# Last product of a hybrid decoder layer: weight sums of twelve of its twenty groups made during the third gating and the up projection and kept in DRAM, with one or two more buffers of each kind

## The chip, the cores and the metric

The kernel runs on one core of a Trainium2 chip. The metric is the device time of one execution in microseconds (us); lower is better. All arithmetic is in float32: a weight or an activation is split into a high part (the value rounded to fp32r, the type that TensorE takes here) and a low part (the rest), and each product is made of three matmuls, high by high, high by low and low by high.

The engines go by the profile's names: PE (TensorE), DVE (VectorE), ACT (ScalarE), POOL (GpSimd), SP (the queue that issues most DMAs).

## The reference

One decoder layer on 256 positions and 2048 channels. An input projection feeds three mixers (A a gated convolution, B a spatial gating, C sparse attention), each with its own output projection and a sigmoid gate; their gated sum goes through `w_o`, a norm and the residual. Then a feed-forward part:

```python
splits = _split_points()
...
    g_a, g_b, g_c = jnp.split(jax.nn.sigmoid(merge_g), 3, axis=-1)
    mixed = (g_a * y_a + g_b * y_b + g_c * y_c) @ w_o[l]
    x = x + rms_norm(mixed, norm_mix_post[l])
    h = rms_norm(x, norm_ffn_pre[l])
    u = causal_depthwise_conv(h @ w_up[l], ffn_conv_w[l], ffn_conv_b[l])
    u_g, u_v = jnp.split(u, 2, axis=-1)
    x = x + rms_norm((jax.nn.silu(u_g) * u_v) @ w_down[l], norm_ffn_post[l])
```

The last product is the one with `w_down`: 256 x 5632 by 5632 x 2048.

## The kernel before

**Stages in order of time:** input projections of the three mixers; gating and output projection of each branch (`branch(0)` for B, `branch(1)` for A, `branch(2)` for C, the "third gating"); the product with `w_o`; the up projection, 88 tiles `f` of 128 features (loop over `NFT`, two tiles a turn); the last product, in two halves of 1024 output columns (`Pair(0)`, `Pair(1)`).

**How a weight gets to PE.** SP loads 128x1024 values (512 KB) into a raw buffer `wraw` (five of them). ACT writes the high part into `whi` (four buffers), DVE subtracts and writes the low part into `wlo` (four buffers). PE then reads both. In the up projection a tile takes two such units, in the gating and in the `w_o` product one unit feeds 12 matmuls.

**The last product.** The 44 feature tiles are 20 in ten pairs (`EARLY`) and 24 alone (`PLAIN`). A plain tile is one unit and 12 matmuls of 128x512 into four PSUM banks `c`. A pair is a "group" (`quad`): one step of a fast matrix product with seven instead of eight block products, for which the four weight blocks of the pair are loaded as `b` and `a` (each 128x1024) and four sums of 128x512 are made of them on DVE, partly in place: `tt[L] = b[L]-a[U]`, `a[U] = a[U]-a[L]`, `tt[U] = b[L]-a[U]`, `b[U] = b[U]-tt[U]`. Then `b`, `a`, `tt` and the upper half of `b` (as `h4`, `l4`, one buffer each) are split, 3.5 units in all, and 21 matmuls follow, into `c` and the four side banks `p1`, `p5`, `p6`, `p7`. The sums of the activations are made ahead, in the up projection (`sums`). `combine` adds the side banks into the result buffer `res`, `result` adds the banks `c`, `weigh` multiplies by the norm's gain.

**What sets the order.** PE's order is set by `in_line`, ACT's and DVE's in the last product by `fixed`: each instruction is issued after the one before it on its engine, in the order of the program text. Elsewhere a scheduler sets the order from priorities; the splits of weights stand ahead of other work (`high_priority`). In `Pair(1)` the last six plain tiles are "kept": their weights are split ahead of time, four of them into buffers of activations no longer needed, and multiplied after everything else, bank by bank, so that each bank's tail (`result`, norm, `weigh`, residual, store) starts early. The residual waits in DRAM (`kept_y`) and is loaded near the end.

Of the kernel before, what the change touches and what calls it, by code (L numbers as in the profile page):

```python
# [30 lines left out]
D = 2048  # L31
T = 256
# [5 lines left out]
EARLY = [(0, 1), (2, 3), (4, 5), (6, 7), (8, 9), (11, 12), (13, 14), (15, 16), (17, 18), (19, 20)]  # L38
PLAIN = [*range(22, 33), 10, 21, *range(33, NFT)]
BA, BB, BC, BG = 2100, 2200, 2200, 2500  # L40
# [14 lines left out]
def block(ctx: ExitStack, tc: tile.TileContext, x, xf, fp, cst, rows, sgw, w1, w2, wf_a, wt_bv, wf_bu, wf_c,  # L55
# [5 lines left out]
    P0 = ctx.enter_context(tc.tile_pool(name="p0", bufs=1))  # L61
    PS = ctx.enter_context(tc.tile_pool(name="ps", bufs=4, space=PSUM))
# [192 lines left out]
    PZ.tile([128, 112], F32, name="fill")  # L255
# [3 lines left out]
    idn = P0.tile([128, 128], F32, name="idn")  # L259
# [62 lines left out]
    hT = P0.tile([128, KT, 2, T], R, tag="hT", name="hT")  # L322
# [24 lines left out]
    rh = PZ.tile([128, 2], F32, name="rh")  # L347
# [532 lines left out]
    mix = {}  # L880

    def branch(bi, act_of):

        for cb in range(4):
            pg = [PS.tile([128, 512], F32, tag="acc", name=f"pg{bi}{cb}{t}") for t in range(2)]
            for q in range(4):
                hs = granule(wt_g[(bi * 4 + cb) * 4 + q])
                for k in range(4 * q, 4 * q + 4):
                    hi, lo = hs[(k % 4) // 2]
                    c = slice((k % 2) * 512, (k % 2) * 512 + 512)  # L890
                    for t in range(2):
                        ts = slice(t * 128, t * 128 + 128)
                        mm_t(pg[t], hT[:, k, 0, ts], hT[:, k, 1, ts], hi[:, c], lo[:, c], k == 0, k == KT - 1)
                if q < 3:
                    pump(BUDGET)
# [9 lines left out]
            for q in range(2):  # L905
# [7 lines left out]
                for k in range(4 * q, 4 * q + 4):  # L913
                    hi, lo = hs[(k % 4) // 2]
                    c = slice((k % 2) * 512, (k % 2) * 512 + 512)
                    for t in range(2):
                        ts = slice(t * 128, t * 128 + 128)
                        mm_t(py[t], act[:, k, 0, ts], act[:, k, 1, ts], hi[:, c], lo[:, c], k == 0, k == 7)
                if q == 0:
# [28 lines left out]
    branch(2, lambda: Ct_box["t"])  # L948
    mh, ml = mix["h"], mix["l"]
# [10 lines left out]
    ss2 = PZ.tile([128, 2, 4], F32, tag="ss8", name="ss2")  # L960
# [72 lines left out]
    h2k = P0.tile([128, 4, 2, 1024], R, tag="hT", name="h2k")  # L1033
# [10 lines left out]
    for n, (cb, p) in enumerate(HELD):  # L1044
        for i in range(2):
# [4 lines left out]
            if (n, i) == (3, 1):  # L1050
                h2 = P0.tile([128, KT, 2, T], R, tag="hT", name="h2T")
# [79 lines left out]
    sums_of = [P2.tile([128, 2, 5, 3, 128], R, name="se")]  # L1131
    gh = [P2.tile([128, 11, T], R, tag="gh", bufs=4, name=f"gh{i}") for i in range(4)]
# [7 lines left out]
    rb2 = junk.bitcast(F32)  # L1140
    ones2 = small("ones2", (128, 128))
# [27 lines left out]
    def sums_at(j):  # L1169
        return sums_of[j // 5][:, 0, j % 5], sums_of[j // 5][:, 1, j % 5]  # L1170

# [30 lines left out]
    for i in range(NFT):  # L1202
        acc = []
        for v in range(2):
            f = 2 * i + v
            with tc.issue_after(pe_last[0]):
                pu = pu2[f] if f < 3 else ftile(wf_up[f], h2)
            s = P2b.tile([128, T], F32, tag="fs", bufs=2, name=f"fs{f}")
            fsum(pu, s, rb=rb2)
            a = small(f"fa{f}")  # L1210
# [21 lines left out]

    P2c = ctx.enter_context(tc.tile_pool(name="p2c", bufs=1))
    fin = P0.tile([128, 7168], F32, tag="hT", name="fin")
    res = fin[:, 0:4096].rearrange("p (t n) -> p t n", t=2)
    gain = fin[:, 4096:5120]
    turn = [0]

    def scratch():
        turn[0] ^= 1  # L1240
        return fin[:, 5120 + 1024 * turn[0]:6144 + 1024 * turn[0]]

    ss3 = PZ.tile([128, 2, 8], F32, name="ss3")
# [12 lines left out]
    def weights(src, into=None):  # L1256
        raw = fetch(src, 1024)
        hi, lo = (into[:, 0], into[:, 1]) if into is not None else ring(raw.name)
        high(hi, raw)
        rest(lo, raw, hi)  # L1260
        return hi, lo

    def ring(name):
        return P0.tile([128, 1024], R, tag="whi", bufs=4, name=f"whi{name}"), rests(f"wlo{name}")[:, 0:1024]

    class Pair:
# [27 lines left out]
        def quad(self, j):  # L1294

            k0, k1 = EARLY[j]
            last = j == len(EARLY) - 1
            b, a = (fetch(wt_dq[self.p, j][:, x:x + 1024], 1024) for x in (0, 1024))
            L, U = slice(0, 512), slice(512, 1024)
            nm = f"q{self.p}_{j}"  # L1300
            tt = scratch()
            (hb, lb), (ha, la), (ht, lt) = (ring(nm + x) for x in "bat")
            h4, l4 = (P2c.tile([128, 512], R, tag=tag, name=f"{tag}{nm}") for tag in ("h4", "l4"))
            high(hb, b)
            fixed(V, V.tensor_sub, tt[:, L], b[:, L], a[:, U])
# [3 lines left out]
            fixed(V, V.tensor_sub, tt[:, U], b[:, L], a[:, U])  # L1309
            high(ht, tt)  # L1310
            rest(la, a, ha)
            fixed(V, V.tensor_sub, b[:, U], b[:, U], tt[:, U])
            high(h4[:, L], b[:, U])
            rest(lt, tt, ht)
            rest(l4[:, L], b[:, U], h4[:, L])
            sh, sl = sums_at(j)
            s1, s2, s4 = ((sh[:, i], sl[:, i]) for i in range(3))
            for bank_, act, (h, l), c in (
                    (self.c[0][1], s4, (hb, lb), L), (self.c[0][0], g2(k1, H1), (hb, lb), U),
                    (self.p1, g2(k0, H1), (ha, la), L), (self.p5, s1, (ha, la), U),  # L1320
                    (self.p7, g2(k0, H2), (ht, lt), L), (self.p6, s2, (ht, lt), U),
                    (self.c[1][0], g2(k1, H2), (h4, l4), L)):
# [34 lines left out]
    NP, NQ, KEEP = len(PLAIN), len(EARLY), 6  # L1357


    first, second = Pair(0), None  # L1360
    i = 0
    for j in range(NQ):
        while i < 3 + (NP - 6) * j // (NQ - 1):
            first.plain(i)
            i += 1
        first.quad(j)
    for i in range(i, NP):
        first.plain(i)
    first.combine()
    second = Pair(1)  # L1370
    kept = []
    i = 0
    for j in range(NQ):
        while i < 3 + (NP - KEEP - 3) * j // (NQ - 1):
# [158 lines left out]
```

## Time and profile before

| | us |
|---|---|
| median of 3 runs | 1564.04 (1563.71 to 1564.49) |
| the profiled execution | 1564.15 |
| its span | 1562.4 |

The page gives each engine's busy time, the chain of work that ended last, and groups of instructions by line. Further views: the chain in order of time; windows (for each stretch its length, then PE, PEld, DVE, ACT and POOL busy us with the number of instructions, the clock granted to PE as a share of full speed, the DMA engines' busy share and GB/s); groups by line (busy us, mean ns of one, idle time just before and what ended it); DMA issues (queue, count, size, median us from issue to landing).

The stages by the chain and the groups: `branch(2)`'s output projection (`py<-whi,Ct`) runs from 631 to 751 us, the up projection's tiles from 877 to 1324 in the chain, the first half of the last product starts at 1325.7, the second at 1438.6. DVE's busy share by fifths of the page's forty slices:

```profile
PE   9999999999999999999999999999999999999997
DVE  7899999857866555465567998888888888888997
```

One digit is the busy share of a fortieth of the span in tenths. DVE is least busy in the middle, from about 430 to 820 us, where the gatings and the `w_o` product run.

### The profile page before, as it was taken

To read this page: it belongs to the slowest core of one execution; us is meant where nothing else is said; L and a number is where in the kernel's file an instruction comes from. 1 tells how busy PE (TensorE), PEld (TensorE's weight loads), DVE (VectorE), ACT (ScalarE), POOL (GpSimd) and SP (SyncE) were. 2 spreads that over 40 slices of the span, in tenths; PEclk is the share of its full clock that TensorE was granted. 3 is DMA by queue.
4 is the path that set the end of the run, shared out by engine and by line. 5 is a ranking of instruction groups with operands and counts; after the bars stand their busy time and mean duration, and the time that the engine had idled before them with its cause. 6 is when DMAs were issued, how large, how long until landed. Compare 5 with 4: busy or idle time off the path is not lost.

```text
span 1562.4 us, 22642 instructions
## 1 busy us (share of the span) xinstructions
PE 1551.2 (99%) x8178; PEld 1316.5 (84%) x8178; DVE 1244.8 (80%) x2370; ACT 889.3 (57%) x1442; POOL 19.2 (1%) x50
## 2 busy tenths in 40 slices
PE   9999999999999999999999999999999999999997
PEld 7888889888888787788888888888888888888885
DVE  7899999857866555465567998888888888888997
ACT  7654454447646675644455665565555555555663
POOL 1000020000000000000000000000000000000000
PEclk9999999999999999999999999999999999999999
DMA  9565556666764445466774666666666666666674
GB/s 377 182 197 185 193 177 215 197 192 180 234 201 161 151 147 169 156 189 188 243 245 144 215 193 196 195 190 196 191 190 197 194 193 195 200 208 202 215 236 156
DMA packets 85441, 307.96 MB, mean 197 GB/s; under 512 B 9808, under 2 KB 10832, under 8 KB 84304
## 3 DMA queue, kind: packets, MB, share of 16 engines
q1 hardware_dynamic: 83376, 297.84, 60.0%
q0 software_dynamic: 1520, 8.39, 1.5%
q8 instruction: 64, 1.05, 0.3%
q14 instruction: 49, 0.40, 0.1%
q10 hardware_dynamic: 432, 0.28, 0.1%
HBM read 301.23 MB, written 4.19 MB: 195 GB/s over the span
## 4 chain that ended last, share of the span: by engine, by line
PE 96%; DVE 2%; DMA 1%; issue 0%; ACT 0%; DVEq 0%; POOL 0%; ACTq 0%; POOLq 0%
PE ps L190 29%; PE ps L197 15%; PE pg L211 6%; PE pg L210 6%; PE pg L212 6%; PE pd0b L1282 5%; PE pd1a L1282 4%; PE py L211 3%; PE py L212 3%; PE py L210 3%; PE po L210 2%; PE po L211 2%; PE po L212 2%; PE pd0a L1282 2%; PE pd1b L1282 1%; PE pv L210 1%
## 5 line engine op out<-in xcount | busy, mean ns | idle before, releaser
L149 ACT ACTIVATE whi<-wraw 128x1024 fp32r<-128x1024 f32 x440 | 461.9, 1054 | 250.8 <-PE pg L212 95.8
L151 DVE TENSOR_TENSOR wlo<-wraw,whi 128x1024 fp32r<-128x1024 f32 (+1 forms) x187 | 226.4, 1216 | 156.5 <-ACT whi L149 155.8
L163 DVE TENSOR_TENSOR wlo<-wraw,whi 128x896 fp32r<-128x896 f32 (+1 forms) x506 | 325.8, 685 | 12.1 <-ACT whi L149 7.3
L190 PE MATMUL ps<-h2T,whi 128*128 128x512 f32 x1360 | 323.1, 389 | 0.0
L190 PEld LDWEIGHTS ps<-h2T,whi 128*128 128x128 f32 x1360 | 249.2, 188 | 46.8
L197 PEld LDWEIGHTS ps<-h2T,wlo 128*128 128x128 f32 x1360 | 167.0, 188 | 6.7
L197 PE MATMUL ps<-h2T,wlo 128*128 128x256 f32 x1360 | 168.9, 277 | 0.0
L190 PE MATMUL ps<-hT,whi 128*128 128x512 f32 x640 | 156.6, 391 | 0.0
L212 PE MATMUL pg<-whi,hT 128*128 128x512 f32 x384 | 150.9, 393 | 0.0
L211 PE MATMUL pg<-wlo,hT 128*128 128x512 f32 x384 | 150.7, 392 | 0.0
L232 ACT ACTIVATE t<-ps 128x256 f32<-128x256 f32 x125 | 47.4, 380 | 175.9 <-PE ps L190 175.9
L210 PE MATMUL pg<-whi,hT 128*128 128x512 f32 x384 | 147.3, 393 | 0.0
L190 PEld LDWEIGHTS ps<-hT,whi 128*128 128x128 f32 x640 | 115.8, 188 | 21.1
L493 DVE SCALAR_TENSOR_TENSOR cv<-hb,fps,cv 128x256 f32<-128x256 f32 x240 | 104.2, 475 | 0.0
L233 DVE TENSOR_TENSOR t<-ps,t 128x256 f32<-128x256 f32 x125 | 52.6, 421 | 50.4 <-ACT t L232 50.4
L197 PEld LDWEIGHTS ps<-hT,wlo 128*128 128x128 f32 x640 | 82.0, 188 | 4.5
L211 PEld LDWEIGHTS pg<-wlo,hT 128*128 128x128 f32 x384 | 72.1, 188 | 16.2 <-issue 1.1
L212 PEld LDWEIGHTS pg<-whi,hT 128*128 128x128 f32 x384 | 72.1, 188 | 15.1 <-issue 0.7
L197 PE MATMUL ps<-hT,wlo 128*128 128x256 f32 x640 | 84.3, 278 | 0.0
L210 PEld LDWEIGHTS pg<-whi,hT 128*128 128x128 f32 x384 | 71.8, 188 | 14.8 <-issue 0.3
L998 DVE TENSOR_TENSOR wlowraw<-wraw,whiwraw 128x1024 fp32r<-128x1024 f32 x44 | 53.2, 1222 | 11.6 <-ACT whiwraw L998 10.2
L998 ACT ACTIVATE whiwraw<-wraw 128x1024 fp32r<-128x1024 f32 x44 | 45.7, 1055 | 18.0 <-PE pd0b L1282 15.0
(1021 smaller groups left out, 2517.3 us busy)
## 6 DMA issues: line engine op xcount, KB each, us to landing
wraw<-in_wf_up_dram SPq DMA_DIRECT2D x176, 512.0 KB, 4.4
wraw<-in_wt_g_dram SPq DMA_DIRECT2D x96, 512.0 KB, 4.3
wraw<-in_wt_p_dram SPq DMA_DIRECT2D x48, 512.0 KB, 3.8
wraw<-in_wt_dn_dram SPq DMA_DIRECT2D x48, 512.0 KB, 4.2
wraw<-in_wt_dq_dram SPq DMA_DIRECT2D x40, 512.0 KB, 4.5
wraw<-in_wf_a_dram SPq DMA_DIRECT2D x32, 512.0 KB, 4.2
wraw<-in_wt_o_dram SPq DMA_DIRECT2D x32, 512.0 KB, 4.6
wraw<-in_wf_bu_dram SPq DMA_DIRECT2D x16, 512.0 KB, 3.9
```

Of the source, the lines that this page charges most:

```text
L149: S.activation(hi[:, :n], raw[:, :n], AF.Copy)
L151: V.tensor_sub(lo[:, :n], raw[:, :n], hi[:, :n].bitcast(F32))
L163: V.tensor_sub(*x)
L190: ins = PE.matmul(ps[:, :, ts], lhsT=ws[k // 8][0][:, c:c + 128], rhs=mov[:, k, :, ts], start=(k == 0 and not t), stop=(k == n - 1), skip_ ...
L197: ins = PE.matmul(ps[:, 1, ts], lhsT=ws[k // 8][1][:, c:c + 128], rhs=mov[:, k, 0, ts], start=False, stop=False, skip_group_check=True).ins
L210: PE.matmul(ps, lhsT=xh, rhs=hi, start=first, stop=False)
L211: PE.matmul(ps, lhsT=xh, rhs=lo, start=False, stop=False)
L212: return PE.matmul(ps, lhsT=xl, rhs=hi, start=False, stop=last).ins
L233: V.tensor_add(t1 if rb is not None else dst, ps[:, 0], t1)
L493: V.scalar_tensor_tensor(ca[:, j], hb[:, j, k:k + T], w(j, k), ca[:, j], op0=ALU.mult, op1=ALU.add)
L998: seq[eng] = [op(*args, **kw).ins]
L1282: ins = PE.matmul(bank, lhsT=a[x], rhs=w[y], start=first and j == 0, stop=last and j == 2).ins
```

## The change

For twelve of the twenty groups (five of the first half, seven of the second; letter Y in the strings below, Q is a group as before) the four sums are made earlier by `weight_sums`: POOL loads the group's blocks `b` and `a` into a buffer, DVE makes the four sums there, POOL writes them to a DRAM tile `made` (2560 columns a group). Eight groups are done in `branch(2)`, one buffer `wsum`, a step of the generator twice a granule; four in the up projection, two buffers (`early`, in place of activation tiles filled later), a step of both at every third tile. Two copies of one column per group, from a tile just written, hold the loads back until that point of the program. In the last product a made group is loaded as four pieces (three of 512 KB, one of 256), split like plain tiles, with no sums.

Besides: one more raw buffer, one more `whi` and one more `wlo` (in the space of `h2T`, on the right side of the memory, where `hT`, `idn`, `res` and the gain now lie), two scratch tiles in place of two halves of one tile, and the order of plain tiles, groups, results and kept tiles written out as the strings `FIRST` and `SECOND`.

```diff
+FIRST = "PPPYPPQPPYPPPQPPYPPQPPYPPQPPYPPQPP"
+SECOND = "PPPRRRRWPYWPPQWPWPYGPPQPPYPPQKPYKPYKPYKBPYKK"
+MADE = [(p, j) for p, steps in enumerate((FIRST, SECOND)) for j, c in enumerate(c for c in steps if c in "QY") if c == "Y"]
...
+    made = tc.dram_tile([max(len(MADE), 1), 128, 2560], F32, name="made")
+
+    def weight_sums(quads, room):
+
+        for n in quads:
+            p, j = MADE[n]
+            y = room(n)
+            L, U = slice(0, 512), slice(512, 1024)
+            b, a, t = y[:, 0:1024], y[:, 1024:2048], y[:, 2048:2560]
+            for x in (b, a):
+                V.tensor_copy(x[:, 0:1], now[0][:, 0:2].bitcast(F32)[:, 0:1] if now[0] is junk else now[0][:, 0:1].bitcast(F32))
+            G.dma_start(b, wt_dq[p, j][:, 0:1024])
+            G.dma_start(a, wt_dq[p, j][:, 1024:])
+            yield
+            yield
+            V.tensor_sub(t, b[:, L], a[:, U])
+            G.dma_start(made[n, :, 1024:1536], t)
+            yield
+            V.tensor_sub(a[:, U], a[:, U], a[:, L])
+            G.dma_start(made[n, :, 0:1024], a)
+            yield
+            V.tensor_sub(b[:, L], b[:, L], a[:, U])
+            yield
+            V.tensor_sub(b[:, U], b[:, U], b[:, L])
+            G.dma_start(made[n, :, 1536:], b)
+            yield
+            yield
...
+                if bi == 2:
+                    next(making, None)
+                    next(making, None)
...
+    making = [weight_sums(range(MIXER + x, len(MADE), 2), lambda n: early[(n - MIXER) % 2]) for x in range(2)]
...
+            if (2 * i + v) % 3 == 0:
+                for steps in making:
+                    next(steps, None)
...
+    raws_of = cycle(tagged("wraw", 5, F32) + [spare(2)])
+    whi = cycle(tagged("whi", 4, R) + [spare(0)])
+    wlo = cycle([lambda name, dt=R: rests(name)[:, 0:1024]] * 4 + [spare(1)])
+    scratch = cycle([extra(0)] + [extra(1)])
...
         def quad(self, j):
...
+            if (self.p, j) in MADE:
+                m = made[MADE.index((self.p, j))]
+                b, a, t = (weights(x) for x in (wt_dq[self.p, j][:, 0:1024], m[:, 0:1024], m[:, 1024:2048]))
+                return self.seven(j, b, a, t, split(load(m[:, 2048:], 512)[:, 0:512], (fourth("h4"), fourth("l4"))))
```

P is a plain tile, R a result, W a `weigh`, G the load of the gain, K a kept tile, B the load of the residual. PE's instructions are the same in number and kind.

**In the order of the instructions.** First DVE in the third gating, at the third of the eight groups (`wsum` is the buffer of the sums, `wlo` the low part of a weight unit, `Ct` the output of mixer C). Before:

```order
L151 TENSOR_TENSOR wlo_6350<-wraw_6347,whi_6349 128x1024
L151 TENSOR_TENSOR wlo_6356<-wraw_6353,whi_6355 128x1024
L151 TENSOR_TENSOR wlo_6386<-wraw_6383,whi_6385 128x1024
L151 TENSOR_TENSOR wlo_6392<-wraw_6389,whi_6391 128x1024
L151 TENSOR_TENSOR wlo_6422<-wraw_6419,whi_6421 128x1024
L845 TENSOR_TENSOR Ct<-O_5651,Ct 128x4x128
```

And now:

```order
L158 TENSOR_TENSOR wlo_6386<-wraw_6383,whi_6385 128x1024
L898 COPY wsum_6413<-wlo_6386 128x1 x2
L158 TENSOR_TENSOR wlo_6421<-wraw_6418,whi_6420 128x1024
L903 TENSOR_TENSOR wsum_6413<-wsum_6413 128x512
L906 TENSOR_TENSOR wsum_6413<-wsum_6413 128x512
L158 TENSOR_TENSOR wlo_6427<-wraw_6424,whi_6426 128x1024
L909 TENSOR_TENSOR wsum_6413<-wsum_6413 128x512
L911 TENSOR_TENSOR wsum_6413<-wsum_6413 128x512
L158 TENSOR_TENSOR wlo_6461<-wraw_6458,whi_6460 128x1024
L852 TENSOR_TENSOR Ct<-O_5657,Ct 128x4x128
```

Two copies and four subtractions now stand between the units' rests; one unit's rest stands between the copies, behind which POOL issues the loads, and the first subtraction, which needs them.

Second POOL at the same group (`made` is the DRAM tile, `rnmp` a row of gains that the `w_o` product's end uses). These rows are new but for `rnmp`, which had only the loads of `x` behind it in this stage:

```order
L912 DMA made<-wsum_6215 128x1024
L1003 DMA rnmp<-in_rows_dram 128x2048
L899 DMA wsum_6413<-in_wt_dq_dram 128x1024
L900 DMA wsum_6413<-in_wt_dq_dram 128x1024
L904 DMA made<-wsum_6413 128x512
L907 DMA made<-wsum_6413 128x1024
L912 DMA made<-wsum_6413 128x1024
```

POOL's queue, nearly empty before, now carries five DMAs a group, and `rnmp` and `x` are issued behind those of the groups ahead.

Third SP in the second half of the last product, where kept tile, plain tile and group follow each other (`in_wt_dn_dram` holds plain and kept tiles, `in_wt_dq_dram` the groups' blocks). Before, with its next kept tile:

```order
L103 DMA wraw_14658<-in_wt_dn_dram 128x1024
L103 DMA wraw_14662<-in_wt_dn_dram 128x1024
L103 DMA wraw_14680<-in_wt_dn_dram 128x1024
L103 DMA wraw_14698<-in_wt_dq_dram 128x1024
L103 DMA wraw_14700<-in_wt_dq_dram 128x1024
L103 DMA wraw_14744<-in_wt_dn_dram 128x1024
```

And now:

```order
L1336 DMA u_14853<-in_wt_dn_dram 128x1024
L1336 DMA u_14857<-in_wt_dn_dram 128x1024
L1336 DMA u_14875<-in_wt_dq_dram 128x1024
L1336 DMA u_14881<-made 128x1024
L1336 DMA u_14887<-made 128x1024
L1336 DMA u_14893<-made 128x512
L1336 DMA u_14921<-in_wt_dn_dram 128x1024
```

A group's two loads became four, three of them from `made`; the one plain tile between two kept tiles takes one load as before.

More of the change, by code (lines that the diff above doesn't have):

```diff
@@ L880, in block @@
     mix = {}
+    made = tc.dram_tile([max(len(MADE), 1), 128, 2560], F32, name="made")
[23 more added lines that the diff above has]
+            yield
+    MIXER = min(len(MADE), 8)
+    making, now = weight_sums(range(MIXER), lambda n: P1.tile([128, 2560], F32, tag="wsum", name=f"wsum{n}")), [None]
     def branch(bi, act_of):
@@ L1131, in block @@
     sums_of = [P2.tile([128, 2, 5, 3, 128], R, name="se")]
+    early = [P2.tile([128, 11 * T], F32, tag=tag, bufs=4, name="made" + tag) for tag in ("gh", "gl")]
     gh = [P2.tile([128, 11, T], R, tag="gh", bufs=4, name=f"gh{i}") for i in range(4)]
@@ L1254, in rest, with cycle, take, spare @@
         fixed(V, V.tensor_sub, lo, x, hi.bitcast(F32))
-    def weights(src, into=None):
[L1257 to L1264, printed above, removed]
+    def cycle(makers):
+        n = [0]
+        def take(name, *args):
+            n[0] += 1
+            return makers[(n[0] - 1) % len(makers)](name, *args)
+        return take
+    def spare(x):
+        return lambda name, dt=R: P2d.tile([128, 1024], dt, tag=f"y{x}", name=name)
+    def extra(x):
+        return lambda name, dt=R: P2c.tile([128, 1024], dt, tag=f"x{x}", name=name)
+    def tagged(tag, bufs, dtype):
+        return [lambda name, dt=dtype: P0.tile([128, 1024], dt, tag=tag, bufs=bufs, name=name)] * bufs
+    raws_of = cycle(tagged("wraw", 5, F32) + [spare(2)])
+    whi = cycle(tagged("whi", 4, R) + [spare(0)])
+    wlo = cycle([lambda name, dt=R: rests(name)[:, 0:1024]] * 4 + [spare(1)])
+    scratch = cycle([extra(0)] + [extra(1)])
+    count = [0]
+    def load(src, n=1024):
+        count[0] += 1
+        to = raws_of(f"u{count[0]}", F32)
+        nc.sync.dma_start(to[:, :n], src)
+        return to
+    def split(x, into=None):
+        hi, lo = into or (whi(f"h{count[0]}"), wlo(f"l{count[0]}"))
+        high(hi, x)
+        rest(lo, x, hi)
+        return hi, lo
+    def weights(src, into=None):
+        return split(load(src), into)
+    def fourth(tag):
+        return P2c.tile([128, 512], R, tag=tag, name=f"{tag}_{count[0]}")
     class Pair:
@@ L1389, in block @@
                 G.dma_start(yb[:, t], kept_y[:, t])
-        for x in range(0 if j < NQ - 5 else 1 if j < NQ - 1 else KEEP - 4):
-            k = NP - KEEP + len(kept)
-            into = None
-            if j < NQ - 1:
-                kt = P2.tile([128, 11, T], R, tag=("gh", "gl")[j % 2], bufs=4, name=f"kept{k}")
-                into = kt[:, 0:8].rearrange("p (a b) c -> p a (b c)", a=2)
-            kept.append((PLAIN[k], weights(wt_dn[1, k], into)))
-    assert i == NP - KEEP and len(kept) == KEEP
+        elif c == "K":
+            keep()
+        else:
+            second.quad(j)
+            j += 1
     second.combine()
+    P2d.tile([128, 120], F32, name="fill2")
     for t in range(2):
```

133 lines of the change are left out of this document (77 added, 56 removed).

## The prediction

> **What bounds the kernel now.** I read the page first, then the chain that ended last in order of time, then the windows of the last product, then the groups by line.
>
> ```profile
> span 1562.4 us, 22642 instructions
> PE 1551.2 (99%) x8178; PEld 1316.5 (84%) x8178; DVE 1244.8 (80%) x2370; ACT 889.3 (57%) x1442; POOL 19.2 (1%) x50
> PE 96%; DVE 2%; DMA 1%; issue 0%; ACT 0%; DVEq 0%; POOL 0%; ACTq 0%; POOLq 0%
> ```
>
> PE is busy in 99% of the span and is 96% of the chain; DVE and DMA share the last 3%. A busy PE may still be waiting inside a matmul whose end is modelled, so I look at the pace. In the chain in order of time (start, length, what, matmuls merged) the last product reads:
>
> ```profile
> 1325.74 9.52 PE pd0b L1282 x42
> 1337.98 7.48 PE pd0b L1282 x33
> ...
> 1438.62 9.52 PE pd1a L1282 x42
> ...
> 1523.55 5.22 DMA wraw<-in_wt_dq_dram
> 1536.40 17.04 PE pd1a L1282 x75
> ```
>
> 9.52/42 and 7.48/33 are both 0.2267 us for one matmul. Each half of the product has 24 plain tiles of 12 matmuls and 10 groups of 21, together 498, so 112.9 us at this pace. The first half runs from 1325.74 to 1438.62, which is 112.88: PE lost nothing there. The second starts at 1438.62 and its last matmul ends at 1553.44, 114.82 later; a last matmul shows about 0.16 beyond its step, so the half lost 114.82 - 0.16 - 112.88 = **1.8 us**. The windows say where (first the length, then each engine's busy us with its count, clock, DMA share, GB/s):
>
> ```profile
> 1460.00:1480.00 20.00, 20.00 (x90) 16.57 (x89) 19.90 (x25) 11.44 (x12) 0.00 (x0) 1.00 0.72 238
> ...
> 1510.00:1520.00 10.00, 10.00 (x46) 8.19 (x45) 8.88 (x11) 5.63 (x7) 0.00 (x0) 1.00 0.78 251
> 1520.00:1530.00 10.00, 9.44 (x42) 7.36 (x41) 8.04 (x10) 5.49 (x6) 0.00 (x0) 1.00 0.69 219
> 1530.00:1540.00 10.00, 9.84 (x42) 7.22 (x41) 9.93 (x13) 5.14 (x6) 1.09 (x2) 1.00 0.19 53
> 1540.00:1550.00 10.00, 10.00 (x46) 8.29 (x45) 5.54 (x14) 3.34 (x8) 0.00 (x0) 1.00 0.41 170
> ```
>
> Two windows hold 42 matmuls where the neighbours hold 46: 8 x 0.2267 is again 1.8 us. Ahead of them DVE is busy for 19.90 of 20 us, and the chain runs through DVE and one load of a group's weights: DVE has used up its lead, and the load was issued late because its buffer was held by the sums made in place. What can be won by relieving DVE in this product is therefore 1.8 us, 0.1%. From PE's end at 1553.44 the span has 9.0 us more, in instructions that the change leaves as they are.
>
> **The change, part by part.** All durations are of the profiled execution: 1564.15 us, span 1562.4; the median of the runs is 1564.04, 0.1 lower.
>
> PE's matmuls are the same in number, kind and, but for some transposes of the third gating, order: no gain and no loss of its own.
>
> *DVE and ACT in the product.* The rows (mean ns of one, then idle before):
>
> ```profile
> L998 DVE TENSOR_TENSOR wlowraw<-wraw,whiwraw 128x1024 fp32r<-128x1024 f32 x44 | 53.2, 1222 | 11.6 <-ACT whiwraw L998 10.2
> L998 ACT ACTIVATE whiwraw<-wraw 128x1024 fp32r<-128x1024 f32 x44 | 45.7, 1055 | 18.0 <-PE pd0b L1282 15.0 <-PE ps L190 2.6 <-PE pd0a L1282 0.3
> L998 DVE TENSOR_TENSOR fin<-wraw,wraw 128x512 f32<-128x512 f32 x40 | 27.4, 685 | 3.1 <-DMA wraw<-in_wt_dq_dram 3.0
> ```
>
> A made group loses four subtractions of 0.685 us, 2.7 us; seven of them in the second half take 19.2 us from DVE. For the stretch from 1440 to 1540 that is
>
> ```profile
> 1440.00:1540.00 100.00, 99.28 (x434) 80.73 (x434) 94.83 (x111) 59.97 (x68) 1.09 (x2) 1.00 0.63 203
> ```
>
> a fall from 94.8 of 100 us to 75.6. ACT's work stays. The 1.8 us of PE's wait goes: **-1.8**.
>
> *DMA in the product.* A made group is loaded as three loads of 512 KB and one of 256 instead of two of 512: 0.79 MB more, 12 times. What is late next is therefore a transfer, and the place is the end of the second half, where plain tile, made group and kept tile follow each other four times: 2.75 MiB = 2.88 MB in 33 matmuls, 7.48 us, so 385 GB/s (before, 2.10 MB, 280 GB/s). The nearest rows for what the queues can give:
>
> ```profile
> 12.00:16.00 4.00, 4.00 (x20) 3.30 (x19) 4.00 (x10) 3.93 (x9) 0.00 (x0) 1.00 1.04 416
> ...
> wraw<-in_wt_dq_dram SPq DMA_DIRECT2D x40, 512.0 KB, 4.5
> ...
> wraw<-in_wt_bv_dram SPq DMA_DIRECT2D x15, 512.0 KB, 7.1
> ...
> 1481.33 0.33 SPq L103 DMA_DIRECT2D wraw<-in_wt_dq_dram  x1
> ```
>
> SP issues 24 more, 0.33 us each where nothing is waited for: 8 us of SP's time in 228, hidden by its waits for buffers.
>
> At 416 GB/s a period takes 6.9 us and costs nothing. The lower end: the window at 1510 moved 251 GB/s at a share of 0.78, so 322 at a full share, if packets kept that length; a period then takes 8.96, 1.5 too long, 5.9 over four. Landing gives another: six raw buffers serve six loads a period, so a buffer may be held for 7.48 us; issue to landing 4.5, ACT 1.05 and DVE 1.22 make 6.8. With the 7.1 of the row that was taken at 416 GB/s it is 9.4, 1.9 too long, 7.6 over four. Against this stands the lead: with five split buffers PE has four more units (2.72 and three of 1.36, 6.8 us) when one is freed, and 2.3 us refill it, so 4.5 us. The cost lies between nothing and 3.1 with the lead, 7.6 without it. I take **0**, since 416 is the row in which the queues were really full.
>
> The Trainium skill, "DMA: Bandwidth & Descriptors", Specifications, states about 358 GB/s as the limit from HBM for one core. By it a period takes 8.06 us, 0.57 too long, 2.3 over the four, which the lead would cover, and 1564.6 if it did not. The row above, with one core running, shows 416.
>
> *Buffers at the product's start.* The moved tiles change no instruction, but the sixth raw buffer and the fifth split pair lie where `h2T` lay, so the first load into them, the third piece of the first group, is issued only when PE leaves the up projection, at 1325.7; SP's next loads, of the second group, queue behind it, as they did behind `gain`. Landing, ACT and DVE make 6.8 us; PE reads that piece after three plain tiles and two pieces, 3 x 2.72 + 2 x 1.36 = 10.9. Covered; without those tiles ahead, 6.8. I take **0**.
>
> *Third gating, eight groups.* Each adds four subtractions, two copies of one column, five issues on POOL, 1.05 MB read and 1.31 MB written.
>
> ```profile
> 700.00:800.00 100.00, 100.00 (x450) 82.81 (x450) 54.27 (x64) 46.52 (x60) 1.08 (x2) 1.00 0.66 207
> L210 PE MATMUL py<-whi,Ct x64: 388/389/397, 631.3 to 751.3; 128*128 128x512 f32 x64
> 1555.65 0.16 DVE L247 RECIPROCAL rsyd<-rsyd 128x1 f32<-128x1 f32 x1
> 633.06 0.57 POOL L956 DMA_DIRECT2D rnmp<-in_rows_dram  x1 [233.71 <-PE s L766]
> rnmp<-in_rows_dram POOLq DMA_DIRECT2D x1, 1024.0 KB, 6.6
> x<-in_x_dram POOLq DMA_DIRECT2D x2, 1024.0 KB, 8.5
> L149 ACT ACTIVATE whi<-wraw 128x1024 fp32r<-128x1024 f32 x440 | 461.9, 1054 | 250.8 <-PE pg L212 95.8 <-PE py L212 51.0 <-PE ps L190 24.3
> L151 DVE TENSOR_TENSOR wlo<-wraw,whi 128x1024 fp32r<-128x1024 f32 (+1 forms) x187 | 226.4, 1216 | 156.5 <-ACT whi L149 155.8
> ```
>
> With a copy at 0.16 (the trace has none of this form; bounds 0 and the 0.685 of the subtraction) a group costs DVE 3.1 us, 24.5 in all, in a stage of some 145 us (96 gate matmuls, 21.8 us, ahead of 631.3, to 752) where DVE is busy for 54%: free by rate. Bytes: 18.9 MB more in 145 us are 130 GB/s on 207, below 416. The danger is the wait: DVE takes its work in order, and the first subtraction waits for loads that POOL issues only after the copies. Two issues of 0.57 and 6.6 us to landing make 7.7 us (9.6 with 8.5), and by the order of the third group only one unit's rest, 2.7 us of PE's pace, stands between: DVE may stand still for 5.0 (6.9). Queued behind it is the next rest (`wlo`), for which PE waits. The lead: whi is refilled when PE frees it (ACT waits for PE in the row above), three more units are 8.2 us, less 1.05 and 1.22 is 5.9 us. So nothing, or 1.0 at the worst landing, for that one group; the others have two or more units between. Without the lead it would be the 5.0. I take **0**.
>
> The loads of `rnmp` and `x` now queue on POOL behind made groups:
>
> ```profile
> 752.46 1.08 POOL L954 DMA_DIRECT2D x<-in_x_dram  x2 [118.83 <-DVE mg L926]
> 830.97 0.54 POOL L1166 DMA_DIRECT2D kept_y<-y  x1 [77.44 <-DVE y L988]
> ```
>
> Their reader has made `y` by 830.97, 78 us after `x` was issued, so some 10 us of delay cost nothing.
>
> *Up projection, four groups:* 12.2 us of DVE within its first 42 tiles.
>
> ```profile
> 877.72:894.08 16.36, 16.36 (x97) 14.47 (x96) 16.19 (x40) 12.55 (x23) 0.00 (x0) 1.00 0.61 181
> ...
> 992.24:1008.60 16.36, 16.36 (x97) 14.47 (x96) 14.97 (x34) 9.74 (x17) 0.00 (x0) 1.00 0.63 192
> ```
>
> The first eight subtractions (5.5 us) fall where DVE is full anyway, 16.19 of 16.36. PE kept its 97 matmuls there all the same, since the rests stand ahead of the work that trails. At most two subtractions, 1.4 us, stand ahead of one tile's rests. Bounds 0 and 5.5; I take **0**, nearest to the row in which a full DVE cost PE nothing.
>
> *Sum:* 1564.15 - 1.8 = 1562.35; against the median 1564.04 - 1.8 = 1562.24. I say **1562.3 us**.
>
> **The rivals.**
> *No gain (1564.1).* The chain's wait at 1523.55 is a DMA of 5.22 us; if landing rather than DVE paced the second half, PE loses the same 1.8 again. Against it: DVE at 19.90 of 20 us just ahead, and one more raw buffer, freed earlier.
> *The transfers take over at the end, lead kept:* up to 3.1, less the 1.8 won: 1563.0 to 1565.4.
> *The transfers take over and the lead is gone (slower):* it decides at a landing of 5.2 us (7.48 - 2.27) in the last 35 us; at 7.1 and without the lead it costs 7.6: 1562.3 + 7.6 = 1569.9, from 1567.2 on if half the lead is left. For it: 385 of 416 GB/s. Against: before the dense part the demand is only 244 GB/s, four plain tiles, a made and an unmade group (4.98 MB in 20.4 us), so all buffers are full when it begins.
> *DVE's wait for POOL's loads stops PE in the third gating:* 1 us or more for several groups, 1563.5 to 1567. Against: the 5.9 us of lead.
>
> **How the numbers follow.** Forecast 0.66 (its own range 1561.9 to 1562.9); no gain 0.13; transfers with the lead 0.07; transfers without it 0.07; gating 0.05; faster 0.02. The measurement can tell 0.2%, 3.1 us, from no change, so faster starts below 1560.9 and slower above 1567.2. Faster needs more than all of PE's loss in the product; the 0.02 is for what the trace cannot show of PE's pace. Slower: 0.07 and a little of the gating, 0.08. Same: 0.90. The range 1561.4 to 1565.5 holds the forecast, no gain and the milder transfers; it leaves out some 0.12.
>
> **What would show it.** Right: all windows of the second half with PE's full count, its DVE near 76% instead of 95%, the last matmul some 1.8 us earlier relative to 1438.62, and the tail of 9.0 us unchanged. The DMA step is wrong if landings in the last 35 us exceed 5.2 us and PE waits for ACT or DMA there. The gating step is wrong if DVE's wait for a weight sum is followed by PE waiting for a rest. Everything is wrong if PE's start of the product moves from 1325.7 by more than 1 us.

## The result, and the profile after

| | before | after |
|---|---|---|
| median, us | 1563.88 (6 runs, 1562.40 to 1564.49) | 1573.95 (6 runs, 1570.47 to 1575.27) |
| profiled execution, us | 1564.15 | 1575.15 |
| its span, us | 1562.4 | 1573.3 |

The changed kernel is slower: ratio 1.0064, 95% interval 1.0051 to 1.0077. The prediction said 1562.3, with 1561.4 to 1565.5 as its range.

The page of the changed kernel, with the span and each engine's busy time:

```profile
span 1573.3 us, 22925 instructions
PE 1556.4 (99%) x8178; PEld 1320.3 (84%) x8178; DVE 1242.1 (79%) x2394; ACT 891.2 (57%) x1442; POOL 52.6 (3%) x110
```

PE's 8178 matmuls are the same, and its busy time has grown by 5 us only, the span by 11. First I look for the stage. The view by tile gives the first and the last start of each kind of matmul; `pd0b` opens the first half of the last product and `pd1a` the second (changed kernel):

```profile
L1367 PE MATMUL pd0b<-h,gh x111: 388/389/396, 1337.2 to 1450.6; 128*128 128x512 f32 x111
L1367 PE MATMUL pd1a<-h,gh x97: 389/389/389, 1451.3 to 1563.5; 128*128 128x512 f32 x97
L1367 PE MATMUL pd1a<-h,gl x97: 388/389/389, 1451.7 to 1563.9; 128*128 128x512 f32 x97
```

The first half starts at 1337.2 instead of 1325.6: **11.6 us are lost ahead of the product**. It takes 1451.3 - 1337.2 = 114.1 instead of 112.9, so 1.2 are lost in it. From the second half's first start to its last lie 112.6 us, where 497 steps of 0.2267 make 112.7: nothing is lost there, and the 1.8 us of before are won. 11.6 + 1.2 - 1.8 = 11.0, and the spans differ by 10.9.

The first matmul of the third gating's output projection starts where it did (631.5 us, before 631.3). The last one of the `w_o` product does not. First the changed kernel, then the kernel before:

```profile
L219 PE MATMUL po<-kept,ml x12: 392/394/397, 833.0 to 853.2; 128*128 128x512 f32 x12
```

```profile
L212 PE MATMUL po<-kept,ml x12: 392/394/397, 821.4 to 841.6; 128*128 128x512 f32 x12
```

So the 11.6 us are lost between, in the third gating and, where the eighth group's sums are made, in the first part of the `w_o` product. This is the timeline of DVE there (start, length, line, operation, count, and in brackets the idle time before and what ended it):

```profile
737.02 2.36 DVE L158 TENSOR_TENSOR wlo<-wraw,whi 128x1024 fp32r<-128x1024 f32 x2
747.00 0.69 DVE L903 TENSOR_TENSOR wsum<-wsum 128x512 f32<-128x512 f32 x1 [7.62 <-DMA wsum<-in_wt_dq_dram]
747.73 0.69 DVE L906 TENSOR_TENSOR wsum<-wsum 128x512 f32<-128x512 f32 x1
748.33 1.22 DVE L158 TENSOR_TENSOR wlo<-wraw,whi 128x1024 fp32r<-128x1024 f32 x1
...
755.73 0.21 DVE L898 COPY wsum<-wlo 128x1 f32<-128x1 f32 x2 [2.58 <-DMA made<-wsum]
...
759.47 1.09 DVE L974 TENSOR_TENSOR mac<-mac,mg 128x256 f32<-128x256 f32 x3
766.62 0.69 DVE L903 TENSOR_TENSOR wsum<-wsum 128x512 f32<-128x512 f32 x1 [6.06 <-DMA wsum<-in_wt_dq_dram]
767.23 1.22 DVE L158 TENSOR_TENSOR wlo<-wraw,whi 128x1024 fp32r<-128x1024 f32 x1
768.37 0.42 DVE L974 TENSOR_TENSOR mac<-mac,mg 128x256 f32<-128x256 f32 x1
```

At the seventh group DVE stands for 7.62 us in front of the first subtraction (L903) until the group's loads land; behind it wait a second subtraction and the rest `wlo`. At the eighth it first waits 2.58 us to write into the one `wsum` buffer, whose seventh group is still on its way to DRAM, and then 6.06 us for the loads; behind that wait a `wlo` and the fourth addition of `mac`. PE in the same stretch (its timeline, columns as above):

```profile
749.61 0.50 PE L218 MATMUL py<-wlo,Ct 128*128 128x512 f32 x1 [1.79 <-DVE wlo L158]
...
750.87 0.48 PE L217 MATMUL py<-whi,Ct 128*128 128x512 f32 x1
751.15 0.63 PE L218 MATMUL py<-wlo,Ct 128*128 128x512 f32 x1
...
754.74 0.39 PE L218 MATMUL py<-wlo,Ct 128*128 128x512 f32 x1
...
768.84 0.69 PE L984 MATMUL pm<-idn,mac 128*128 128x128 f32 x2 [3.94 <-DVE mac L974]
769.18 0.78 PE L217 MATMUL po<-whi,mh 128*128 128x512 f32 x1
...
775.14 0.39 PE L219 MATMUL po<-whi,ml 128*128 128x512 f32 x1
```

PE stands 1.79 us for the `wlo` and 3.94 us for `mac`, which are just the two instructions queued behind DVE's waits. And after each stop it goes on at half speed for a while: most starts are 0.42 to 0.43 us apart instead of 0.227, at 0.63 us a matmul instead of 0.39. The windows give the clock (length; PE, PEld, DVE, ACT, POOL busy with counts; clock; DMA share; GB/s):

```profile
751.00:754.00 3.00, 3.00 (x9) 2.35 (x8) 2.15 (x2) 0.48 (x1) 0.53 (x1) 0.50 0.97 313
...
764.00:769.00 5.00, 1.06 (x5) 0.56 (x5) 2.38 (x4) 0.00 (x0) 0.55 (x1) 0.91 1.00 415
769.00:775.00 6.00, 6.00 (x16) 4.74 (x17) 6.00 (x10) 1.72 (x3) 1.07 (x2) 0.51 0.95 341
```

And in the kernel before:

```profile
751.00:754.00 3.00, 3.00 (x15) 2.49 (x14) 3.00 (x8) 1.07 (x1) 1.08 (x2) 1.00 0.66 213
...
769.00:775.00 6.00, 6.00 (x28) 4.95 (x27) 3.01 (x4) 2.91 (x5) 0.00 (x0) 1.00 0.57 186
```

The granted clock is 0.50 and 0.51 instead of 1.00, and PE counts as busy all the same: that is most of the 5 us by which its busy time grew. From 750.87 to 754.74 PE starts ten matmuls later, 3.87 us where 2.27 would do (1.6 lost); from 769.18 to 775.14 fourteen, 5.96 where 3.17 would do (2.8 lost). So of the 11.6 us the two waits are 5.7 and the half clock after them 4.4; the remaining 1.5 are smaller pieces that were not traced one by one.

### The profile page after: what moved, and what is told of

It is laid out like the page before. It is cut to its first block, busy times and chain, and to the rows that moved or that the text cites. A ratio compares the mean times of both kernels' runs of the same rounds, so it can differ in the third digit from the quotient of the medians.

```text
span 1573.3 us, 22925 instructions
## 1 busy us (share of the span) xinstructions
PE 1556.4 (99%) x8178; PEld 1320.3 (84%) x8178; DVE 1242.1 (79%) x2394; ACT 891.2 (57%) x1442; POOL 52.6 (3%) x110
## 3 DMA queue, kind: packets, MB, share of 16 engines
q8 instruction: 64, 1.05, 0.3%
## 5 line engine op out<-in xcount | busy, mean ns | idle before, releaser
L1045 DVE TENSOR_TENSOR l<-u,h 128x1024 fp32r<-128x1024 f32 (+1 forms) x100 | 109.5, 1116 | 37.4 <-ACT h L1045 35.3
L1045 ACT ACTIVATE h<-u 128x1024 fp32r<-128x1024 f32 (+1 forms) x100 | 94.5, 971 | 54.6 <-PE pd0b L1367 14.2
```

The source lines that it names most:

```text
L1045: seq[eng] = [op(*args, **kw).ins]
```

## The experiments

Theory A: DVE stands still in order at a group's first subtraction until the loads land, and what is queued behind it comes late for PE. Theory B: the groups' bytes, in flight with the weights, make these late. Theory C: the time is lost elsewhere. The kernel before ran beside every set; its median was 1562.9 to 1563.1 us. All ratios are to it, with 95% intervals.

**Seven groups in the gating**, the eighth in the up projection.

```
-    MIXER = min(len(MADE), 8)
+    MIXER = min(len(MADE), 7)
```

> The eighth group goes from the third gating to the up projection; the seventh stays where it was. Theory A (DVE stands still in order in front of a group's first subtraction until POOL's loads land, and whatever is queued behind it comes late for PE): the stop at 768.8 us (4.10 us, DVE's sum `mac` for the transposes, and some 15 matmuls at half clock after it, 2.9 us) goes, the one at 749.6 (1.95 us, and 1.6 us at half clock) stays: about 7 us less than with eight, so some 3 to 4.5 us slower than the kernel before (1567.0 to 1568.5). Theory B (the groups' bytes slow the weight loads of the whole stage, each group by its share): an eighth of the loss goes, some 9 us slower than before (1573). Theory C (the loss arises in the up projection or in the product): no gain, or worse, as the up projection has one group more: 1574 or above.

Measured: 1567.49 us (1565.45 to 1570.43), ratio 1.0033 (1.0022 to 1.0043). C falls. The stop at 768 is gone, as A said. The one at 749, which A left in place, is not there in the execution that was profiled, the fastest of this run, because the loads landed in 8.0 us instead of 9.65 (timeline of DVE):

```profile
745.07 0.69 DVE L903 TENSOR_TENSOR wsum<-wsum 128x512 f32<-128x512 f32 x1 [5.83 <-DMA wsum<-in_wt_dq_dram]
```

A wait of 5.83 us on DVE costs PE nothing, one of 7.62 cost it 1.79; in two runs below 6.27 cost about 0.4 and 7.12 about 1.1. The lead that the prediction worked out, 5.9 us, holds to within some 0.2 us. The runs lie 5 us apart, and those of the kernel before about 2.

**Six groups in the gating** (the same line with 6).

> Groups seven and eight go to the up projection. Theory A: both stops go, and with them the half clock; the six earlier groups never stopped PE. What stays is the product: 1.8 us less in its second half, 1.1 us more at its start. 1563 to 1564, that is 0.0 to 1.5 us less than the kernel before, if six groups in the up projection cost nothing there. Theory B: two eighths of the loss go, some 8 us slower than before (1572). Theory C: no gain, or worse, 1574 or above.

Measured: 1565.65 us (1563.46 to 1567.93), ratio 1.0017 (1.0008 to 1.0026). Most of the loss is gone, but not all: 2.6 us above the kernel before, not level. In this trace PE loses nothing in the gating worth naming, but the product's first half runs from 1326.1 to 1441.7 us, 115.6 instead of 112.9, a loss of 2.7. A second cause, then; it is taken up below.

**Seven groups, with the seventh's first subtraction later in DVE's order.**

```
             yield
             yield
+            if n == 6:
+                yield
+                yield
+                V.tensor_copy(t[:, 0:1], now[0][:, 0:1].bitcast(F32))
             V.tensor_sub(t, b[:, L], a[:, U])
```

> As with seven groups in the third gating, but one copied column more holds the seventh group's first subtraction back until the rest of the last granule, two rests later in DVE's order; its loads are issued where they were, and all bytes stay. Theory A: DVE's wait of 7.6 us for these loads falls to some 2 us, under the lead of 5.9 us, so PE is not stopped at 749.6 any more and its clock stays up: some 3.5 us less than with seven groups alone, 1563 to 1564.5, level with six. Theory B: the same bytes at the same time, so no difference from seven groups alone.

Measured: 1565.59 us (1564.46 to 1568.16), ratio 1.0019 (1.0010 to 1.0028): 1.9 less than with seven groups alone, level with six, but the intervals of the two overlap. The loads were issued at the same place and took as long (736.45 to 745.86, against 737.04 to 745.07), but DVE's wait for them is 1.10 us instead of 5.83. PE is stopped here in neither of the two traces, so this speaks for A but doesn't decide it.

**All eight groups, with the first subtraction of the seventh and the eighth later.** As above, and for the eighth a copied column that follows the fourth addition of `mac`.

```
+            if n == 7:
+                V.tensor_copy(t[:, 0:1], mac[:, 1, D - 1:D])
```

> Eight groups in the third gating with all their bytes; only the places of the first subtractions of the seventh and the eighth in DVE's order move: a copied column more holds the seventh's back until the last granule's rest, the eighth's until the sum `mac` is done. Theory A (DVE's standing still in order): neither stop of PE is left, no window of the gating below a clock of 1.00, and the time is that of six groups in the gating, 1565.6 (2 to 3 us above the kernel before on this chip). Theory B (bytes in flight late for the weights): both stops stay, 1573 to 1575.

Measured: 1566.07 us (1564.30 to 1568.14), ratio 1.0018 (1.0009 to 1.0027), 8 us under the changed kernel's 1573.95 (7 by the ratios). The windows where it stood:

```profile
748.00:751.00 3.00, 3.00 (x15) 2.49 (x14) 1.53 (x2) 1.06 (x1) 0.55 (x1) 1.00 0.79 280
751.00:764.00 13.00, 13.00 (x63) 10.86 (x62) 9.34 (x19) 5.34 (x8) 3.23 (x7) 1.00 0.95 333
764.00:769.00 5.00, 5.00 (x24) 4.14 (x23) 5.00 (x8) 2.13 (x2) 0.00 (x0) 1.00 0.99 404
```

PE is full and its clock 1.00, while the DMA engines are as busy as ever (0.95 and 0.99). DVE still waits for the loads, for the writes too (5.0 and 5.3 us in all), only at places where PE has what it needs. This settles the main cause: not the bytes, not the work, but what stood behind the wait. Some of the loss is left in this trace: the third gating's output projection takes 123.0 us (631.1 to 754.1) instead of 120.0. PE waits there 0.67 us for a `wlo` at 709.23, at the fifth group, where DVE had stood 6.81 us for the loads, and 0.49 for `mac` at 727.25, at the sixth. So the earlier groups, which did not stop PE in the changed kernel's trace, can do it too.

**A group's loads from ACT's queue instead of POOL's**, in the gating.

```
-            G.dma_start(b, wt_dq[p, j][:, 0:1024])
-            G.dma_start(a, wt_dq[p, j][:, 1024:])
+            Q = nc.scalar if n < MIXER else G
+            Q.dma_start(b, wt_dq[p, j][:, 0:1024])
+            Q.dma_start(a, wt_dq[p, j][:, 1024:])
```

> Eight groups again, but the loads of a group in the third gating are issued from ACT's queue, not from POOL's; same bytes, DVE's order as it was but for the sixth group. Theory A with a slow path from POOL (8 to 10 us from issue to landing there, 4.5 to 6.4 for SP's loads of the same size): a landing of 5 to 6.5 us takes 3 to 4 us off both waits of DVE, so the stop at 749.6 goes (7.6 less 3 is under the lead of 5.9) and the one at 768.8 shrinks to 1 or 2 us: 4 to 9 us less than with eight groups from POOL, 1565 to 1570. Theory A with a landing that the bytes in flight set: the landing stays at 8 to 10 us, 1573 or 1574. In both ACT may lose time while it waits for the copies of DVE.

Measured: 1575.26 us (1574.61 to 1576.64), ratio 1.0080 (1.0065 to 1.0095): no gain. The median landing is 7.0 us from ACT's queue and 7.2 from POOL's, where the weights' loads of the same size take 5.1 to 6.2 in the same stretch of the changed kernel. The issuing queue isn't why they are slow. The time of this run measures more than the landing, for ACT, which takes its work in order too, now stood behind the copies itself (from 750.8 to 754.6 us at the eighth group). DVE's wait at the seventh group was 4.80 us here, under the lead, and PE did not stop; at the eighth it was 5.65 and PE stood 5.33 us.

**The loads of `x` after the eighth group's second subtraction.** `last_sum` is a column of the group's first difference.

```
     for t in range(2):
+        V.tensor_copy(x2[:, t, 0:1], last_sum[0])
         G.dma_start(x2[:, t], x[t])
```

> The changed kernel, but the two loads of `x` (2 MB) are issued only after the eighth group's second subtraction; in the changed kernel they follow that group's own loads by 1 us. The seventh group and its stop at 749.6 are untouched. Theory A1 (the landing is set by the bytes in flight together): the eighth group's loads land in 6 to 7 us instead of 10.4, DVE's wait there falls by about 3.5 and PE's stop of 4.1 us at 768.8 to 1 us or less, with half a window of half clock less: 4 to 6 us less than the changed kernel, 1568 to 1570. Theory A2 (a group's loads land in 9 to 10 us whatever else runs): no difference, 1574.

Measured: 1573.85 us (1571.11 to 1576.84), ratio 1.0075 (1.0060 to 1.0090): no difference that can be told. The loads, issued from 753.66 on, were there at 763.10, 9.4 us instead of 10.4, and PE stood 4.27 us for `mac`. So not A1: 2 MB less in flight beside them did not bring the landing to 6 or 7 us. But A2's 9 to 10 us aren't fixed either: in the next run, with `x` behind them as in the changed kernel, the same loads landed in 7.7 us.

**The wait filled.** 36 transposes whose result nothing reads stand ahead of the two that wait for `mac`.

```
             for t in range(2):
+                for _ in range(36 * (k == 14) * t):
+                    PE.transpose(pt[:, 128:256], mac[:, 1, 13 * 128:14 * 128], ident)
                 PE.transpose(pt[:, t * 128:t * 128 + 128], mac[:, t, k * 128:k * 128 + 128], ident)
```

> The changed kernel with 36 transposes more, of a part of `mac` that is ready, set ahead of the two that wait for DVE at 768.8 us; nothing reads them, and at 0.11 us each they fill 4.0 of the 4.1 us in which PE stands there. The stop at 749.6 stays as it is. Theory: the half clock after a stop (15 matmuls at 0.427 us instead of 0.227 in the changed kernel) comes from PE's standing idle: the clock stays at 1.00 from 764 to 776 and the time falls by 2 to 3 us against the changed kernel, 1571 to 1572. Rival (the clock falls for another reason at that place, such as the DMA traffic of 419 GB/s): no difference, 1574.

Measured: 1573.15 us (1572.13 to 1576.40), ratio 1.0071 (1.0055 to 1.0086). The times overlap with those of the changed kernel, so the 2 to 3 us that were expected aren't measured. The trace answers the question (PE's timeline, then the windows):

```profile
762.42 4.09 PE L985 MATMUL pm<-idn,mac 128*128 128x128 f32 x36
767.57 0.55 PE L986 MATMUL pm<-idn,mac 128*128 128x128 f32 x3 [1.05 <-DVE mac L974]
```

```profile
764.00:769.00 5.00, 3.95 (x32) 3.53 (x30) 3.65 (x5) 0.66 (x2) 0.87 (x2) 1.00 1.00 392
769.00:775.00 6.00, 6.00 (x28) 4.96 (x27) 5.78 (x10) 2.13 (x2) 0.75 (x2) 1.00 1.01 417
```

PE has to wait until 767.57 as before, but idles 1.05 us of it instead of 3.94, and the clock stays at 1.00: 28 matmuls from 769 to 775, where the changed kernel made 16. DMA is as busy as there. So the half clock after this stop comes from the idling. (The loads landed earlier here, so that without the filling the wait would have been some 5.1 us, from 762.4 to 767.57.)

**Six groups in the gating, and the new buffers late.** The sixth raw buffer and the fifth split pair join their rings only from the third turn on, and `gain` is loaded after the first half's loads are issued.

```
-    def cycle(makers):
-        n = [0]
+    def cycle(makers, late=0):
+        n = [-late * (len(makers) - 1)]
...
-            return makers[(n[0] - 1) % len(makers)](name, *args)
+            m = len(makers) if n[0] > 0 else len(makers) - 1
+            return makers[(n[0] - 1) % m](name, *args)
```

> Six groups in the gating, and in the product the sixth raw buffer and the fifth split pair are used only from the third turn of their rings on, and `gain` is loaded after the first half's loads are issued: no load of the first group waits for PE to leave the up projection. Theory D (the 2.6 us that six groups still cost against the kernel before come from the third piece of the first group: its load is issued at PE's end of the up projection, lands some 7 us later behind `gain`, and ACT and DVE then make the pieces behind it in order, each late): PE's losses of 2.7 us in the first half's first 16 us go, and what stays is the 1.8 us won in the second half: 1.5 to 2 us less than the kernel before, 1561.2 to 1561.6 where that has 1563.0. Rival (DVE and ACT are simply full at that place with the last tiles of the up projection): the loss stays at 2 to 3 us, 1565 to 1566.

Measured: 1563.99 us (1562.52 to 1566.66), ratio 1.0007 (0.9999 to 1.0016): 1.7 less than six groups without it, though the intervals overlap, level with the kernel before, and not the 1.5 to 2 under it. In the trace the loss at the start is gone: the first half takes 112.9 us (window of this run: PE busy for 20 of 20 us):

```profile
1325.00:1345.00 20.00, 20.00 (x92) 16.60 (x91) 15.14 (x21) 10.54 (x14) 0.00 (x0) 1.00 0.79 251
```

So the buffers that come free only when PE leaves the up projection, and what queues behind their loads, are the second cause; whether the buffers or the load of `gain` weighs more isn't shown, since the edit moves both. Part of what is missing from the gain lies ahead of the product, which starts at 1327.0 here: the third gating's output projection takes 121.6 us instead of 120.0. What was missing besides is asked next.

**No group made**: every Y of the two strings is a Q.

```
+FIRST = "PPPQPPQPPQPPPQPPQPPQPPQPPQPPQPPQPP"
+SECOND = "PPPRRRRWPQWPPQWPWPQGPPQPPQPPQKPQKPQKPQKBPQKK"
```

> All twenty groups are summed in the product as in the kernel before; what stays of the change is the product's order and its buffers (sixth raw, fifth split pair, second place for sums). The gating and the up projection are those of the kernel before. If the sums are what took DVE's lead (the prediction's step): PE loses the 1.8 us in the second half, and what the start of the product costs comes on top: 1563 to 1566. If the buffers alone make good the loss: 1.8 less than before, 1561.2, or level where the start costs the same again. The start of the product tells by itself whether its 1 to 2.7 us come from the buffers (then they are lost here too) or from the made group's bytes (then not).

Measured: 1564.04 us (1563.89 to 1564.48), ratio 1.0007 (0.9999 to 1.0016). PE loses 0.7 us at the product's start (the first half takes 113.6 us) and 1.2 in its second half (113.9 from the first start to the last). With the same early buffers and a made first group the start cost 0.6 to 2.8 in the traces, 1.2 in the changed kernel, so the buffers alone don't account for it. The loss in the second half is there without the sums and absent in every trace with them, as the prediction had it; the buffers alone don't win it.

**The kernel before, again**, without an edit.

> The kernel before, once more, with its profile. It tells how far the 1.8 us that PE lost in the second half of the product are the same in every execution. If they are: two windows between 1520 and 1540 with 42 matmuls again, and 1.8 us between the second half's length and 112.9 us. If they come and go (the runs of before lie from 1562.2 to 1564.6): a loss between 0 and 1.8, with a span shorter by as much, and then the change had less to win than the prediction took from one trace.

Measured: 1563.11 us, span 1561.4. The windows of the place where the prediction found its 1.8 us:

```profile
1520.00:1530.00 10.00, 10.00 (x44) 7.99 (x43) 8.55 (x10) 5.71 (x7) 0.00 (x0) 1.00 0.69 226
1530.00:1540.00 10.00, 9.91 (x44) 7.77 (x43) 9.29 (x12) 4.54 (x6) 1.09 (x2) 1.00 0.27 86
```

44 matmuls in each, not 42. From the second half's first start to its last lie 1552.0 - 1438.6 = 113.4 us, 0.7 over 112.7. The loss isn't the same in every execution: 1.8 in one, 0.7 in the other, and with it the span falls by 1.0.

**Six groups, all in the up projection** (the last six of the second half), late buffers, none in the gating.

```
+FIRST = "PPPQPPQPPQPPPQPPQPPQPPQPPQPPQPPQPP"
+SECOND = "PPPRRRRWPQWPPQWPWPYGPPQPPYPPQKPYKPYKPYKBPYKK"
...
+    MIXER = 0
```

> No group is made in the third gating; the last six made groups of the second half are summed in the up projection, all other groups in the product as before; buffers used late as in the run with late buffers. The gating is then that of the kernel before. If theory A holds for what is left of six groups in the gating (small stops that differ from run to run, 1562.5 to 1566.7), the runs lie as close together as those of before, and the product's gain shows by itself: 0.5 to 1.8 us less than before, 1561.2 to 1562.5 where before has 1563.0. If six groups in the up projection cost PE something there, or the product has nothing to win in most runs: 1563 or above.

Measured: 1563.50 us (1563.35 to 1563.97), ratio 1.0004 (0.9995 to 1.0013). The runs lie within 0.6 us of each other, so the spread of 4 to 5 us came with the groups in the gating. The second half loses nothing, the start 0.7, as in the run with no group made, although the buffers are late here: the first group is unmade in both. The time is above the 1561.2 to 1562.5 that was hoped for. The span is 1561.4, that of the kernel before in the run above, yet the execution took 2.0 us more than its span, and that kernel 1.7.

**The first group and the last five, all in the up projection**, late buffers: the pieces that lost nothing, put together. FIRST begins "PPPYPPQ" and is as above from there; SECOND is that of the run above with a Q for its first Y.

> The first group of the product and the last five of the second half are made, all in the up projection; none in the third gating; late buffers. The parts that lost nothing put together: no loss at the product's start (0.6 us with that group unmade), none in the second half (0.6 to 1.8 in the two executions of before), the gating as before. If that adds up: 0.3 to 1 us less than the kernel before, 1562 to 1562.6 where that has 1562.9 or 1563.0. If what lies around the span is longer with the change, as it was with six groups in the up projection (2.0 against 1.75 us): level, 1562.7 to 1563.2.

Measured: 1562.83 us (1562.60 to 1563.20) against 1563.07, ratio 0.9999 (0.9990 to 1.0008). Its span is 1560.7, 0.7 under the shorter one of before, and PE loses nothing in the product. Outside the span are 2.0 us again. No difference that can be measured: the best form of this change breaks even.

## Why the prediction was wrong, step by step

*PE bounds, and 1.8 us are lost in the second half of the product.* Right in mechanism: with the sums made ahead, PE lost nothing there in any trace, and DVE, 94.83 of 100 us before, had room (changed kernel; the half starts 12.7 us later, and so does the window):

```profile
1452.70:1552.70 100.00, 100.00 (x443) 82.81 (x442) 81.33 (x85) 61.87 (x70) 1.08 (x2) 1.00 0.77 268
```

75.6 had been worked out for DVE; it is 81.3. The term itself was read from one execution, and another has 0.7.

*The transfers at the dense end cost 0.* Right:

```profile
1520.00:1530.00 10.00, 10.00 (x46) 8.29 (x45) 8.17 (x8) 6.87 (x8) 0.00 (x0) 1.00 1.01 393
...
u<-made SPq DMA_DIRECT2D x7, 512.0 KB, 5.6
```

393 GB/s, with PE at its full 46 matmuls. The loads landed in 5.3 to 5.7 us there (the second row, for 1510 to 1545), over the 5.2 that was named as the limit; the lead covered it. The Trainium skill, "DMA: Bandwidth & Descriptors", Specifications, has about 358 GB/s as the limit from HBM for one core; the row, with one core running, is above it.

*The buffers at the product's start, "Covered … I take 0".* Wrong, by 1.2 us in the changed kernel and 2.7 with six groups. These are rows of SP's queue, ACT, DVE and PE of the changed kernel:

```profile
1337.43 0.33 SPq L1299 DMA_DIRECT2D gain<-in_rows_dram  x1
1337.81 0.42 SPq L1336 DMA_DIRECT2D u<-made  x1
...
1344.92 1.06 ACT L1045 ACTIVATE h<-u 128x1024 fp32r<-128x1024 f32 x1 [2.55 <-DMA u<-made]
1347.61 0.42 ACT L1279 ACTIVATE gh<-fa 128x256 fp32r<-128x256 f32 x1 [1.63 <-DVE fa L1276]
...
1350.13 2.36 DVE L1045 TENSOR_TENSOR l<-u,h 128x1024 fp32r<-128x1024 f32 x2 [0.25 <-ACT h L1045]
...
1351.41 0.50 PE L1367 MATMUL pd0b<-l,gh 128*128 128x512 f32 x1 [0.50 <-DVE l L1045]
```

The third piece's load goes out behind `gain` and lands 7.1 us later, not the 4.5 of the row that was used. The piece itself is in time. But ACT and DVE take their work in order, so the fourth piece and the next plain tile, and the up projection's own last work between them, are made behind it, and PE waits for those. The step asked whether the late piece comes in time, and not what queues behind it on ACT and DVE.

*The third gating, "So nothing, or 1.0 at the worst landing, for that one group; the others have two or more units between … I take 0".* This is the step that failed. Three things were wrong in it, and one was missing.
- The landing was bounded rightly for the seventh group (7.7 to 9.6; it took 9.65, 737.35 to 747.00), not for the eighth (10.4, 756.20 to 766.62); the lead was right. But two units between were counted as safe, as if each took PE's 2.7 us. DVE had both rests' inputs already and made them in 2.36 us, the row at 737.02. What remains of the landing, 7.6 us, is more than 5.9 by 1.7; PE stood 1.79.
- Only the next rest was looked for behind the wait. At the eighth group the fourth addition of `mac` stood there as well, and for PE's transposes the lead of the rests counts for nothing.
- The one `wsum` buffer made the eighth group's copies wait for the seventh's writes (2.58 us) and so sent its loads out later. That wait had no term.
- Missing was the price of a stop beyond its length: 4.4 us of half clock on 5.7 of waiting.

The rival "DVE's wait for POOL's loads stops PE in the third gating" was the right one, with the sign that was named for it (DVE's wait for a weight sum, then PE's wait for a rest); its 1563.5 to 1567 were too low for the reasons above; the sign for everything being wrong, a start of the product more than 1 us off, came too, at 11.5. And a chance of 0.05 was too little where a bound of 9.6 stood against a lead of 5.9.

*The up projection, four groups, 0.* Right as far as it was measured: with six there and none in the gating the first matmul of the product comes at the same time as before (1325.5 against 1325.6 and 1325.7).

## What to carry to other kernels

Where an engine that works in order is given a wait for a transfer, list everything that stands behind the wait and who needs it, and count the work ahead of it at that engine's own speed, not at the pace of the bound engine. Compare the worst landing, less that work, with the lead; if it is larger at one place, the change costs there, and a stop of the bound engine may cost more than its length, here 1.3 to 1.9 times as much. Take a gain that is read from one execution to be as uncertain as the runs differ.

## What the runs showed of the hardware

PE's clock halves after a stop that is long enough. Idle times of 0.98, 1.05 (both in the run with the filled wait) and 1.40 us (near the start of the run with ACT's queue, at 7.2 us) were followed by no such stretch. After 1.79 us the clock was 0.50 for some 3.4 us, beginning 1.3 us after PE had gone on. After 3.94, 4.27 (the run with `x` later) and 5.33 us (ACT's queue) it was half from the start, for 5.7, 2.7 and 3.6 us: a longer stop did not mean a longer stretch. With it the four stops cost 1.9, 1.7, 1.3 and 1.3 times their length. The Trainium skill, "TensorE: Matmul & The Clock Gate", Part 1, describes a halved clock after at least one idle window of about 3.4 us, and a full one after about 3.4 us of sustained work. The trace agrees in the factor and, in two of the four stretches, in the 3.4 us; but here 1.79 us of idling were enough.

The two loads of a group land in 7.0 us (median) from ACT's queue and 7.2 from POOL's. At the eighth group they took 7.7 to 11.7 us in five executions. Why they take longer than the weights' loads of the same size isn't settled. That loads issued together delay each other fits one row: in the up projection of the changed kernel two groups' loads are issued within 2.2 us, and the first group's land in 6.7 us, the second's in 11.6 (medians). It was not tried apart.
